# A hybrid diffusion step on one core: mixer B's first preparation placed in mixer A's tail, modulation with its weights stationary, substitution in two parts

## The chip, the cores and the metric

The kernel runs on one core of a Trainium2 chip. The metric is the device time of one execution in microseconds; lower is better. One execution was also profiled: that run's time and the span of its trace (first to last instruction) are given beside the runs that were only timed.

## What is computed

Two layers of a diffusion network are applied to a prompt of 128 tokens and a sample of 1024 (9 tiles of 128 tokens), model width 1024, all in fp32. The parts that the change touches belong to the first layer, and its modulation also to the second:

```python
def modulation(cvec, ada_w, ada_b):            # per layer, for the prompt and for the sample
    m = silu(cvec) @ ada_w + ada_b             # ada_w: 1024 x 3072
    return split_cols(m, [D_MODEL] * 3)        # shift, scale, gate

def even_layer(x, shift, scale, gate, ...):
    h = rms_norm(x, norm_pre) * (1 + scale) + shift
    qa, ka, va, ga, pb, gb = split_cols(h @ w_in, ...)
    ya = windowed attention with a sink        # mixer A, 8 heads
    yb = rwkv_mix(pb, ...)                     # mixer B, 8 heads, both directions in time
    y = concat(ya * silu(ga), yb * silu(gb)) @ w_out
    return x + gate * rms_norm(y, norm_post)

def rwkv_scan(S0, r, decay, kk, a, k, v, reverse):
    def step(S, inp):                          # one token
        sa = einsum('bhvk,bhk->bhv', S, -kk_t)
        S = S * w_t + outer(sa, kk_t * a_t) + outer(v_t, k_t)
        return S, einsum('bhvk,bhk->bhv', S, r_t)
```

The second layer is a differential attention over the same tokens.

## The kernel before

Projections are exact to fp32 by splitting operands into a high and a low fp32r part, three matmuls in place of one (L364 to L366, L378 to L380).

**Start.** `mod_chunks` computes the modulation in blocks of 128 of the 3072 columns. One step loads the weights (tiles `adaw`, from `in_ada_w`), then for each block 8 matmuls accumulate over the 1024 rows (L298). Their stationary operand is a 128 wide slice of the silu'd vectors `sc`, of which the first two columns count; the 128 columns of the weights stream past. The result has the vectors along partitions, so ScalarE copies it to SBUF (L300, tile `mrow`, or `raw` for four blocks in mixer A's tail), TensorE transposes it (L304) and VectorE adds the bias (L309 to L313). Sixteen blocks are needed before the first projection, four (`EARLY`) come behind mixer A, and 28 more, as a filler called `mods`, run along mixer B.

**Mixer A** runs in `mixer_a`, interleaved with the projections of `transposed`, whose weights are the tiles `wgh`, `wgl` (pool `wp`, two buffers; the four late modulation blocks use them too); A's own projection weights are `wa`, in the same pool. Its end is `values`: transposes of the probabilities (L652), products (L663, L664) in the bank `po`, and a gated copy (L672).

**Mixer B** cuts the tokens into chunks of 64 and solves each chunk as a triangular system. Work is divided into 9 items: for each of four pairs of heads the first and the second half of the sample's time, then the prompt for all. An item goes through these generators; each `yield` ends a step:

- `b_prep(item, direction)`, 5 steps: loads `low`, `lora` (one buffer each) and four `hb` tiles, two low-rank products (L943), tanh (L950), a running sum of the decay on VectorE (L960, one `tensor_tensor_scan` over 512 columns; the mask `rmask` restarts it every 64), exponentials and products.
- `b_front(item, direction)`, 10 steps, two halves: transposes (L1017), chunk products (L1027), masks (L1033 writes `za`, L1035 writes `q`), products (L1042).
- `b_subst(item)`, 2 steps: GpSimd gathers the diagonal blocks of `za` (L1061, four copies), VectorE transposes them so that columns lie along the free axis (L1062, tile `mp`, 32 columns), then GpSimd substitutes backward, 31 pairs of instructions (L1069, L1071) on the tile `rp`.
- `b_invert(item)`, 8 steps: VectorE transposes `rp` twice (L1077 into `Rt`, L1080), TensorE builds the rest of the inverse and the factors `E`, `VU`.
- `b_scan`: 8 serial steps over the chunks, in each TensorE (L1165), VectorE (L1167), TensorE (L1169), VectorE (L1176), ScalarE (L1178, the new state `S`).
- `b_finish`: normalization and gate, after the second half of each pair.

**What sets the order.** The generators are emitted by `timeline`: each part is given a start and an end in units of the iteration, its steps are spread evenly over them, and they are emitted in order of those times. Iteration i holds the scan of item i, the inversion of i + 1, fronts and substitution of i + 2, and the first preparation of i + 3; `TIMES` has a row for i = -2, i = -1, i = 0 to 4 and the rest, `T7` and `T8` serve the last two. The order of emission is a priority: a list scheduler then places instructions on the in-order queues of the engines by its own model, and may pass an instruction that it thinks is not ready. Tiles of closed pools are reused by later pools; an instruction that first touches such memory waits for the last reader there. SP issues nearly all loads, in its own order.

The four PSUM pools of mixer A lie from bank 0 as projection (2 banks), transposes (3), scores (2), output (1); mixer B's `ps_y` takes three banks from the other end, so its first tiles lie where A's output and scores were.

Of the kernel before, what the change touches and what calls it, by code (L numbers as in the profile page):

```python
# [19 lines left out]
P = 128  # L20
D = 1024
KT = D // P
# [119 lines left out]
def hybrid_step(ctx: ExitStack, tc: tile.TileContext, I, O, stop=99):  # L142
# [95 lines left out]
    def silu2(pool, x, out, tag="sge"):  # L238

        e = tl(pool, [P, x.shape[1]], tag, bufs=2)  # L240
        AE.activation(e, x, AF.Tanh, scale=0.5)
        VE.scalar_tensor_tensor(out, e, 1.0, x, op0=ALU.add, op1=ALU.mult)  # L242
# [33 lines left out]
    silu2(cp, cin, cin)  # L276
# [10 lines left out]
    def mod_chunks(l, c, n, pool, psum, tag, rows, bufs=2, ahead=None, tags=("adaw",) * 2):  # L287
# [36 lines left out]
    def mod_gate(l, psum, tag, rows):  # L324
# [3 lines left out]
        row = rows()[:16, :P]  # L328
# [370 lines left out]
    with ExitStack() as ph1:  # L699
        hp = ph1.enter_context(space("hT0", 1))  # L700
        hh, hl = tl(hp, [P, KT, TOK], "hh", F32R), tl(hp, [P, KT, TOK], "hl", F32R)
        with ExitStack() as su:
            xp = su.enter_context(space("su", 2))
            pt = su.enter_context(space("psut", 3, space=PSUM, side="right"))
            ps = su.enter_context(space("psu", 3, space=PSUM, side="right"))
# [10 lines left out]
            def chunks(j):  # L716
                ahead = []
                for _ in mod_chunks(0, 4 * j, 4, xp, ps, "ps", lambda: tl(xp, [P, P], "mrow"), 4, ahead):
                    pass
                ahead.pop()()  # L720
# [10 lines left out]
            for i in range(3):  # L731
# [20 lines left out]
        rest = transposed(blocks, wp, rp, bp, psum[0], psum[1], hh, hl, ind)  # L752
        run(some(rest, 7), 1, None, 1)
        run(rest, 56, hurried(mixer_a(hh, hl, wp, rp, ap, psum, rope, idb, msk), 1000), 12 * NT * 1)
        for c in range(16, 16 + EARLY):
            run(mod_chunks(0, c, 1, wp, psum[0], "ps", lambda: tl(rp, [P, 1024], "raw")[:, :P], tags=("wgh", "wgl")),
# [111 lines left out]
    NHB = 11  # L868
    ON_VE = ()
# [9 lines left out]
    class Item:  # L879
# [3 lines left out]
        def __init__(s, pairs, start, first=True, last=True):  # L883
            s.pairs, s.start, s.first, s.last = pairs, start, first, last
            s.nl = len(pairs)
            s.steps = 8 // s.nl

# [29 lines left out]
    def b_prep(it, d, pool, pre, ps_y, rmask):  # L917
# [42 lines left out]
        VE.tensor_tensor_scan(G, rmask, G, 0.0, op0=ALU.mult, op1=ALU.add)  # L960
# [89 lines left out]
    def b_subst(it, pool, pre, eye, eng):  # L1050
# [3 lines left out]
        mp, rpb = tl(pre, [P, 32, 32], "mp"), tl(pre, [P, 16, 32], "rp")  # L1054
        tmp = tl(pre, [P, 136], "tmp")
# [6 lines left out]
        VE.transpose(mp.rearrange("p c i -> p (c i)"),  # L1062
                     dg.rearrange("p (o u) c -> p c o u", o=1).to_broadcast([P, 32, 2, 16]))
        yield
        for j in range(31, 0, -1):
            t = j // 2
            n = 16 - t
            tv = tmp[:, :n * j].rearrange("p (t i) -> p t i", i=j)
            eng.tensor_tensor(tv, mp[:, j:j + 1, 0:j].to_broadcast([P, n, j]),  # L1069
                             rpb[:, t:16, j:j + 1].to_broadcast([P, n, j]), ALU.mult)  # L1070
            eng.tensor_tensor(rpb[:, t:16, 0:j], rpb[:, t:16, 0:j], tv, ALU.add)  # L1071
        it.rpb = rpb

    def b_invert(it, Rt, pool, pre, ps_s, ps_a):

        rpb, za = it.rpb, units(it)
# [174 lines left out]
    with ExitStack() as ph2:  # L1251
# [8 lines left out]
        ps_y = early.enter_context(space("bpy", 3, space=PSUM, side="right"))  # L1260
        ps_a = early.enter_context(space("bpa", 1, space=PSUM, side="right"))
        ps_s = ph2.enter_context(space("bps", 2, space=PSUM))
        ps_b = ph2.enter_context(space("bpb", 1, space=PSUM))
# [16 lines left out]
        rmask = tl(bc, [P, 512], "rmask")  # L1280
# [584 lines left out]
```

## Time and profile before

| | us |
|---|---|
| runs that were timed | 2103.79, 2097.02, 2094.81 (median 2097.02) |
| the profiled execution | 2095.15 |
| its span | 2093.3 |

| engine | busy, us | share of the span | instructions |
|---|---|---|---|
| TensorE, matmuls | 1966.0 | 94% | 15196 |
| TensorE, weight loads | 1789.1 | 85% | 15196 |
| VectorE | 1483.8 | 71% | 3758 |
| ScalarE | 1071.1 | 51% | 2856 |
| GpSimd | 685.6 | 33% | 951 |

TensorE's mean granted clock is 0.981 of full speed. The engines run side by side, each through its own queue in order; a busy share over the whole span is a mean over stages with different limits. In the rows below PE is TensorE's matmuls, PEld its weight loads, DVE VectorE, ACT ScalarE, POOL GpSimd, SPq the queue that issues loads.

### The profile page before, as it was taken

To read this page: it belongs to the slowest core of one execution; us is meant where nothing else is said; L and a number is where in the kernel's file an instruction comes from. 1 tells how busy PE (TensorE), PEld (TensorE's weight loads), DVE (VectorE), ACT (ScalarE), POOL (GpSimd) and SP (SyncE) were. 2 spreads that over 40 slices of the span, in tenths; PEclk is the share of its full clock that TensorE was granted. 3 is DMA by queue.
4 is the path that set the end of the run, shared out by engine and by line. 5 is a ranking of instruction groups with operands and counts; after the bars stand their busy time and mean duration, and the time that the engine had idled before them with its cause. 6 is when DMAs were issued, how large, how long until landed. Compare 5 with 4: busy or idle time off the path is not lost. (4 is left out here: it accounts for less than half of the span.)

```text
span 2093.3 us, 40906 instructions
## 1 busy us (share of the span) xinstructions
PE 1966.0 (94%) x15196; PEld 1789.1 (85%) x15196; DVE 1483.8 (71%) x3758; ACT 1071.1 (51%) x2856; POOL 685.6 (33%) x951
## 2 busy tenths in 40 slices
PE   7899999999779999998998999999999999999998
PEld 7899999999668888777777888999998999898786
DVE  5355567565756777867468677888888878887867
ACT  4433345343546555655356565555555555555643
POOL 1232232331176766656123222222222221212204
PEclk9999999999989999989999999999999999999999
DMA  7512233111654555433466410010101010101325
GB/s 288 162 62 74 65 96 104 63 56 50 201 168 150 162 165 156 138 113 120 156 213 232 144 37 29 31 31 28 32 28 40 20 45 15 50 10 48 105 66 177
DMA packets 165080, 205.72 MB, mean 98 GB/s; under 512 B 16369, under 2 KB 108049, under 8 KB 164881
## 3 DMA queue, kind: packets, MB, share of 16 engines
q1 hardware_dynamic: 162016, 198.25, 29.7%
q10 hardware_dynamic: 2864, 4.85, 0.7%
q8 instruction: 120, 1.97, 0.4%
q14 instruction: 80, 0.65, 0.1%
HBM read 152.32 MB, written 50.74 MB: 97 GB/s over the span
## 5 line engine op out<-in xcount | busy, mean ns | idle before, releaser
L1539 ACT ACTIVATE p<-s,mx 128x384 f32<-128x384 f32 (+1 forms) x400 | 225.1, 572 | 122.1 <-DVE mx L1536 99.7
L1534 DVE TENSOR_REDUCE mc<-s 128x1 f32<-128x384 f32 x384 | 204.7, 552 | 28.5 <-PE s L1532 25.0
L364 PE MATMUL ps<-wch,hh 128*128 128x384 f32 x576 | 205.0, 357 | 1.8 <-ACT wch L270 0.7
L1532 PE MATMUL s<-kst,qs 128*128 128x384 f32 x768 | 194.9, 353 | 10.1 <-ACT p L1539 9.7
L365 PE MATMUL ps<-wcl,hh 128*128 128x384 f32 x576 | 198.8, 345 | 4.7 <-POOL wcl L271 4.7
L366 PE MATMUL ps<-wch,hl 128*128 128x384 f32 x576 | 196.4, 341 | 2.7 <-DVE hl L1684 2.7
L411 POOL TENSOR_TENSOR q<-ropea,ropeb 128x256 f32<-128x256 f32 x56 | 44.1, 787 | 444.9 <-DVE ropeb L408 304.3
L378 PE MATMUL ps<-hh,wgh 128*128 128x384 f32 x504 | 173.4, 344 | 7.0 <-DVE bo L242 5.9
L379 PE MATMUL ps<-hl,wgh 128*128 128x384 f32 x504 | 172.5, 342 | 0.1
L380 PE MATMUL ps<-hh,wgl 128*128 128x384 f32 x504 | 171.5, 341 | 0.0
L1069 POOL TENSOR_TENSOR tmp<-mp,rp 128x126 f32<-128x126 f32 (+22 forms) x279 | 133.3, 478 | 63.2 <-DVE mp L1062 39.9
L1532 PEld LDWEIGHTS s<-kst,qs 128*128 128x128 f32 x768 | 127.3, 189 | 24.4 <-ACT p L1539 17.1
L271 POOL TENSOR_TENSOR wgl<-raw,wgh 128x1024 fp32r<-128x1024 f32 (+1 forms) x39 | 74.9, 1923 | 217.1 <-ACT wgh L270 216.9
L1071 POOL TENSOR_TENSOR rp<-rp,tmp 128x126 f32<-128x126 f32 (+22 forms) x279 | 129.5, 464 | 21.9
L1415 ACT CAST ah<-pt 128x512 fp32r<-128x512 f32 (+2 forms) x168 | 86.2, 533 | 79.2 <-PE pt L1570 77.1
L1416 DVE TENSOR_TENSOR al<-pt,ah 128x512 fp32r<-128x512 f32 (+2 forms) x168 | 100.7, 615 | 32.1 <-ACT ah L1415 30.8
L365 PEld LDWEIGHTS ps<-wcl,hh 128*128 128x128 f32 x576 | 109.2, 190 | 7.8 <-POOL wcl L271 7.3
L364 PEld LDWEIGHTS ps<-wch,hh 128*128 128x128 f32 x576 | 109.3, 190 | 5.9 <-DVE vl L1416 2.4
L366 PEld LDWEIGHTS ps<-wch,hl 128*128 128x128 f32 x576 | 109.1, 189 | 3.4 <-DVE hl L1684 3.4
L378 PEld LDWEIGHTS ps<-hh,wgh 128*128 128x128 f32 x504 | 94.9, 188 | 9.0 <-DVE bo L242 6.8
L271 POOL TENSOR_TENSOR wcl<-raw,wch 128x512 fp32r<-128x512 f32 x54 | 76.0, 1415 | 81.2 <-ACT wch L270 81.1
L1552 DVE SCALAR_TENSOR_TENSOR p<-p,lr,p 128x1152 f32<-128x1152 f32 (+1 forms) x72 | 98.9, 1374 | 0.4
(472 smaller groups left out, 5759.1 us busy)
## 6 DMA issues: line engine op xcount, KB each, us to landing
hb<-pbT SPq DMA_DIRECT2D x90, 256.0 KB, 4.1
adaw<-in_ada_w_dram SPq DMA_DIRECT2D x56, 256.0 KB, 3.7
raw<-in_wc_dram SPq DMA_DIRECT2D x48, 256.0 KB, 2.7
adaw<-in_ada_w_dram SPq DMA_DIRECT2D x8, 1024.0 KB, 10.5
pbT<-bm SPq DMA_DIRECT2D x16, 512.0 KB, 2.7
low<-lowT SPq DMA_DIRECT2D x16, 512.0 KB, 4.7
raw<-in_wo_dram SPq DMA_DIRECT2D x32, 256.0 KB, 2.8
raw<-in_wpb_dram SPq DMA_DIRECT2D x13, 512.0 KB, 3.6
```

The source lines that it names most:

```text
L271: eng.tensor_tensor(lo[:, j:j + w], raw[:, :w], hi[:, j:j + w].bitcast(F32), ALU.subtract)
L364: PE.matmul(ps[:, :n], hh[:, k, s], wh[:, k], start=k == 0, stop=False)
L365: PE.matmul(ps[:, :n], hh[:, k, s], wl[:, k], start=False, stop=False)
L366: PE.matmul(ps[:, :n], hl[:, k, s], wh[:, k], start=False, stop=k == KT - 1)
L378: PE.matmul(ps[:, :THIRD], wh[:, k], hh[:, k, s], start=k == 0, stop=False)
L379: PE.matmul(ps[:, :THIRD], wh[:, k], hl[:, k, s], start=False, stop=False)
L380: PE.matmul(ps[:, :THIRD], wl[:, k], hh[:, k, s], start=False, stop=k == KT - 1)
L1069: eng.tensor_tensor(tv, mp[:, j:j + 1, 0:j].to_broadcast([P, n, j]), rpb[:, t:16, j:j + 1].to_broadcast([P, n, j]), ALU.mult)
L1071: eng.tensor_tensor(rpb[:, t:16, 0:j], rpb[:, t:16, 0:j], tv, ALU.add)
L1532: PE.matmul(s[c][:, :w], qs[:, e, z], hd.kp[:, z] if own else hd.kst[:, z, w * c:w * c + w], start=e == 0, stop=e == 1)
L1534: VE.tensor_reduce(mc[:, c:c + 1] if nb > 1 else mx, s[c][:, :w], axis=AX.X, op=ALU.min)
L1539: AE.activation(e[:, w * c:w * c + w], s[c][:, :w], AF.Exp, scale=-1.0, bias=mx, accum_out=sums[:, z, c:c + 1])
```

## The change

1. `mod_chunks` swaps its operands: the weights become stationary and the slice of `sc` streams. The result stands with its columns along partitions, and the copy and the transpose go.
2. Mixer A's PSUM pools change places, the projection weights of `transposed` and of the late modulation blocks get a pool `wq` below A's `wa`, the start's PSUM pools move to the other side, and the first preparation of B (item 0, direction 0) gets two banks of its own, where the projections' banks were. B's other PSUM pools are opened behind it.
3. `b_subst` is cut in two: 24 of the 32 columns are transposed and substituted first, the other 8 columns have their own transpose, and their 7 pairs of steps are emitted when the item's inversion begins or the next item's substitution starts its steps, whichever is emitted first. `rp` gets two buffers.
4. The running sum of the decay is made in four pieces of 128 columns, and its mask is 128 wide.
5. `TIMES`, `T7` and `T8` get new values.

```diff
-            pr = tl(psum, [P, 512], tag)[:, 0:P]
+            ps = tl(psum, [P, 512], tag)
             for k in range(KT):
-                PE.matmul(pr, sc[:, 2 * k:2 * k + P], w[k // 4][:, k % 4, P * i:P * i + P], start=k == 0, stop=k == KT - 1)
-            row = rows()
-            AE.copy(row, pr)
-
-            def finish(i=i, row=row):
-                ps = tl(psum, [P, 512], tag)[:, 0:P]
-                PE.transpose(ps, row, ident)
-                ps = ps[:, 0:2]
+                PE.matmul(ps[:, 0:P], w[k // 4][:, k % 4, P * i:P * i + P], sc[:, 2 * k:2 * k + P], start=k == 0,
+                          stop=k == KT - 1)
+
+            def finish(i=i, ps=ps[:, 0:2]):
...
-            pt = su.enter_context(space("psut", 3, space=PSUM, side="right"))
-            ps = su.enter_context(space("psu", 3, space=PSUM, side="right"))
+            pt = su.enter_context(space("psut", 3, space=PSUM))
+            ps = su.enter_context(space("psu", 3, space=PSUM))
...
+        wq = ph1.enter_context(space("wq", 2))
         wp = ph1.enter_context(space("wp", 2))
         psum = [ph1.enter_context(space(n, b, space=PSUM))
-                for n, b in (("ppr", 2), ("ptr", 3), ("psc", 2), ("ppo", 1))]
+                for n, b in (("psc", 2), ("ppo", 1), ("ptr", 3), ("ppr", 2))]
+        psum = psum[3], psum[2], psum[0], psum[1]
...
-        rest = transposed(blocks, wp, rp, bp, psum[0], psum[1], hh, hl, ind)
+        rest = transposed(blocks, wq, rp, bp, psum[0], psum[1], hh, hl, ind)
...
+    SPLIT = 8
...
-        VE.tensor_tensor_scan(G, rmask, G, 0.0, op0=ALU.mult, op1=ALU.add)
+        for x in range(0, 512, P):
+            VE.tensor_tensor_scan(G[:, x:x + P], rmask, G[:, x:x + P], 0.0, op0=ALU.mult, op1=ALU.add)
...
+        it.rpb = rpb = tl(pre, [P, 16, 32], "rp", bufs=2)
...
+        def columns(a, b):
+            m = tl(pre, [P, b - a, 32], f"mp{a}")
+            VE.transpose(m.rearrange("p c i -> p (c i)"),
+                         dg[:, :, a:b].rearrange("p (o u) c -> p c o u", o=1).to_broadcast([P, b - a, 2, 16]))
+            return m
+
+        def steps(m, a, b):
+            for j in range(b - 1, max(a, 1) - 1, -1):
+                t = j // 2
+                n = 16 - t
+                tv = tl(pre, [P, 136], "tmp")[:, :n * j].rearrange("p (t i) -> p t i", i=j)
+                eng.tensor_tensor(tv, m[:, j - a:j - a + 1, 0:j].to_broadcast([P, n, j]),
+                                 rpb[:, t:16, j:j + 1].to_broadcast([P, n, j]), ALU.mult)
+                eng.tensor_tensor(rpb[:, t:16, 0:j], rpb[:, t:16, 0:j], tv, ALU.add)
+
+        high_columns = columns(SPLIT, 32)
+        yield
+        if it.before is not None:
+            it.before.last_steps()
+        low_columns = columns(0, SPLIT)
+        steps(high_columns, SPLIT, 32)
+        it.pending = lambda: steps(low_columns, 0, SPLIT)
+        yield
 
     def b_invert(it, Rt, pool, pre, ps_s, ps_a):
 
+        it.last_steps()
...
-        run(prep(0, 0), 1, None, 1)
+        with space("bpp", 2, space=PSUM, side="right") as ps_p:
+            for d in range(1):
+                run(b_prep(items[0], d, pool, fr, ps_p, rmask), 1, None, 1)
+        ps_y = early.enter_context(space("bpy", 3, space=PSUM, side="right"))
...
```

Each row of `TIMES` lists scan, inversion, finish, front 0, preparation 1, front 1, substitution, next preparation 0, the number of modulation steps and their time:

```diff
-        T7, T8 = ((-0.45, 0.93), (0.92, 1.54), (-0.16, 0.18)), (0.15, 0.54)
+        T7, T8 = ((-0.71, 0.77), (0.92, 1.55), (-0.2, 0.14)), (0.41, 0.8)
         TIMES = (
-            ((0.17, 0.93), (0.38, 1.09), (0.04, 0.46), (0.11, 0.32), (0.03, 0.3), (0.39, 0.75), (0.84, 0.85), (0.55, 1.18), 3, (0.04, 0.97)),
-            ((-0.17, 0.69), (0.79, 1.09), (-0.04, 0.37), (0.22, 0.32), (0.09, 0.4), (0.36, 0.72), (0.78, 0.79), (0.8, 1.29), 12, (0, 1)),
-            ((-0.01, 0.85), (0.6, 1.52), (-0.04, 0.48), (0.04, 0.32), (0.1, 0.38), (0.36, 0.69), (0.73, 0.83), (0.73, 1.23), 8, (0.0, 1.0)),
-            ((-0.16, 0.85), (0.48, 1.51), (-0.07, 0.44), (0.04, 0.32), (0.07, 0.38), (0.34, 0.71), (0.84, 0.96), (0.54, 1.16), 8, (0.01, 1.02)),
+            ((0.17, 1.0), (0.38, 1.09), (-0.04, 0.46), (0.11, 0.32), (0.05, 0.3), (0.39, 0.78), (0.84, 0.85), (0.55, 1.18), 4, (0.05, 0.97)),
+            ((-0.17, 0.69), (0.79, 1.09), (-0.04, 0.37), (0.22, 0.32), (0.09, 0.4), (0.36, 0.79), (0.78, 0.79), (0.64, 1.29), 12, (-0.31, 0.93)),
+            ((-0.05, 0.85), (0.6, 1.63), (0.27, 0.75), (0.04, 0.32), (0.1, 0.38), (0.36, 0.64), (0.79, 0.8), (0.54, 1.24), 7, (0.01, 0.97)),
+            ((-0.2, 0.85), (0.48, 1.62), (0.21, 0.71), (0.04, 0.32), (0.07, 0.38), (0.34, 0.66), (0.83, 0.84), (0.35, 1.17), 6, (0.02, 0.94)),
```

## Rows read from the trace of the kernel before

**Rows 1.** Busy time by stretch: PE, PEld, DVE, ACT, POOL, granted clock, DMA share, GB/s

```profile
60.00:540.00 480.00, 468.32 (x2924) 449.36 (x2923) 278.48 (x684) 189.97 (x434) 129.25 (x104) 1.00 0.27 88
540.00:634.00 94.00, 68.79 (x788) 57.52 (x786) 61.08 (x117) 44.43 (x119) 47.92 (x102) 0.85 0.58 181
634.00:983.00 349.00, 320.65 (x4545) 278.50 (x4544) 261.73 (x579) 200.41 (x521) 223.67 (x459) 0.97 0.46 142
983.00:1100.00 117.00, 112.70 (x888) 89.94 (x888) 71.49 (x169) 52.15 (x115) 31.09 (x48) 0.99 0.57 182
```

**Rows 2.** Timeline and one stretch around the end of mixer A

```profile
539.63 1.06 PE L298 MATMUL ps<-wgl,prm 128*128 128x128 f32 x8
...
540.71 0.59 SPq L929 DMA_DIRECT2D low<-lowT  x1
...
549.59 1.16 PE L943 MATMUL py<-low,lora 128*128 128x512 f32 x4 [1.97 <-DVE gt L672]
...
550.78 0.54 SPq L929 DMA_DIRECT2D low<-lowT  x1
...
556.39 2.05 PE L943 MATMUL py<-low,lora 128*128 128x512 f32 x4 [5.64 <-DMA lora<-loraT]
...
540.00:550.00 10.00, 6.21 (x33) 4.02 (x32) 8.34 (x21) 3.17 (x10) 1.17 (x2) 1.00 0.51 145
```

**Rows 3.** Timeline, item 0 from its substitution to its first state, all engines

```profile
577.09 3.29 POOL L1061 COPY hb<-za 32x512 f32<-32x512 f32 x4 [23.31 <-DVE za L1033]
...
613.15 0.23 POOL L1071 TENSOR_TENSOR rp<-rp,tmp 128x16 f32<-128x16 f32 x1
613.45 2.56 POOL L1061 COPY hb<-za 32x512 f32<-32x512 f32 x4
...
616.04 1.93 DVE L1062 STREAM_TRANSPOSE mp<-hb 128x1024 f32<-128x1024 f32 x1 [1.58 <-POOL hb L1061]
617.89 0.67 DVE L1080 STREAM_TRANSPOSE hb<-Rt 128x512 f32<-128x512 f32 x1
...
616.08 0.47 PE L304 MATMUL py<-cst,mrow 128*128 128x128 f32 x1 [8.42 <-ACT mrow L300]
...
634.26 0.68 ACT L1178 ACTIVATE S<-G,D 128x128 f32<-128x128 f32 x2
```

**Rows 4.** Busy time by stretch, two items of seven, from first state to first state

```profile
634.00:679.00 45.00, 43.24 (x651) 38.62 (x651) 31.37 (x67) 27.29 (x73) 27.64 (x56) 1.00 0.44 131
...
930.00:983.00 53.00, 46.28 (x623) 37.04 (x623) 41.99 (x99) 30.07 (x79) 36.94 (x80) 0.97 0.42 129
```

**Rows 5.** Groups of instructions, 634 to 983 us: busy, mean ns | idle before, releasers

```profile
L1069 POOL TENSOR_TENSOR tmp<-mp,rp 128x56 f32<-128x56 f32 (+22 forms) x216 | 106.5, 493 | 54.2 <-DVE mp L1062 37.9
...
L1061 POOL COPY hb<-za 32x512 f32<-32x512 f32 x28 | 17.0, 608 | 54.3 <-ACT mrow L300 30.1 <-PE sc L1165 8.3 <-ACT S L1178 8.0
```

**Rows 6.** Timeline, VectorE in one item, before the copies of 759.79 and behind

```profile
756.99 1.08 DVE L1077 STREAM_TRANSPOSE Rt<-rp 128x512 f32<-128x512 f32 x1
...
758.83 0.76 DVE L1033 TENSOR_TENSOR za<-pa,cstones 128x256 f32<-128x256 f32 x2
...
764.75 0.41 DVE L1167 TENSOR_TENSOR VU<-VU,sc 64x256 f32<-64x256 f32 x1 [2.66 <-PE sc L1165]
```

**Rows 7.** Timeline, TensorE at the start's last modulation block: start, duration, instruction

```profile
54.92 1.95 PE L298 MATMUL ps<-adaw,prm 128*128 128x128 f32 x16
...
58.00 0.27 PE L304 MATMUL ps<-cst,mrow 128*128 128x128 f32 x1
```

**Rows 8.** One line's instructions (min/median/max ns), then groups of 727 to 880 us

```profile
L304 PE MATMUL py<-cst,mrow x28: 272/328/475, 566.6 to 878.0; 128*128 128x128 f32 x28
...
L960 DVE TENSOR_TENSOR_SCAN hb<-rmask,hb x18: 1210/1225/1364, 551.6 to 941.5; 128x512 f32<-128x512 f32 x18
...
L1033 DVE TENSOR_TENSOR za<-pa,cstones 128x256 f32<-128x256 f32 x24 | 9.3, 417 | 0.8 <-PE pa L1027 0.6
...
L1035 DVE TENSOR_TENSOR q<-pa,cstones 128x512 f32<-128x512 f32 x12 | 8.2, 679 | 0.0
```

More of the change, by code (lines that the diff above doesn't have):

```diff
@@ L236, in some, with silu2 @@
             yield
-    def silu2(pool, x, out, tag="sge"):
-        e = tl(pool, [P, x.shape[1]], tag, bufs=2)
+    def silu2(pool, x, out, bufs=2):
+        e = tl(pool, [P, x.shape[1]], "sge", bufs=bufs)
         AE.activation(e, x, AF.Tanh, scale=0.5)
@@ L275, in hybrid_step @@
     cin = sc[:, :16]
-    silu2(cp, cin, cin)
+    silu2(cp, cin, cin, 1)
     VE.tensor_scalar(cin, cin, 0.5, None, op0=ALU.mult)
@@ L285, in hybrid_step, with mod_chunks @@
     gcol = tl(cp, [P, 2, 2, 8], "gcol")
-    def mod_chunks(l, c, n, pool, psum, tag, rows, bufs=2, ahead=None, tags=("adaw",) * 2):
+    def mod_chunks(l, c, n, pool, psum, tag, bufs=2, ahead=None, tags=("adaw",) * 2):
         w = []
@@ L327, in mod_gate @@
         PE.transpose(pt[:16, :P], gcol[:, l].rearrange("p r c -> p (r c)"), ident)
-        row = rows()[:16, :P]
+        row = rows()
         VE.tensor_copy(row, pt[:16, :P])
@@ L717, in chunks @@
                 ahead = []
-                for _ in mod_chunks(0, 4 * j, 4, xp, ps, "ps", lambda: tl(xp, [P, P], "mrow"), 4, ahead):
+                for _ in mod_chunks(0, 4 * j, 4, xp, ps, "ps", 4, ahead):
                     pass
@@ L886, in __init__, with last_steps @@
             s.steps = 8 // s.nl
+        pending = None
+        def last_steps(s):
+            if s.pending is not None:
+                s.pending()
+                s.pending = None
         def lanes(s, d):
@@ L1278, in ring @@
             return states[n][turn[n] % 3]
-        rmask = tl(bc, [P, 512], "rmask")
+        rmask = tl(bc, [P, P], "rmask")
         GE.memset(rmask, 1.0)
-        GE.memset(rmask[:, 0:512:64], 0.0)
+        GE.memset(rmask[:, 0:P:64], 0.0)
         items = []
@@ L1325, in hybrid_step @@
         for i, it in enumerate(items):
-            it.pool = pools[i % 3]
+            it.pool, it.before = pools[i % 3], items[i - 1] if i else None
             it.done = it.prev.done if not it.first else set()
-        rows = lambda: tl(fr, [P, P], "mrow")
-        T7, T8 = ((-0.45, 0.93), (0.92, 1.54), (-0.16, 0.18)), (0.15, 0.54)
+        rows = lambda: tl(fr, [16, P], "mrow")
+        T7, T8 = ((-0.71, 0.77), (0.92, 1.55), (-0.2, 0.14)), (0.41, 0.8)
         TIMES = (
[4 rows of a table removed]
[4 rows of a table added]
         )
@@ L1340, in mods @@
                 for c in range(a, 24):
-                    yield from mod_chunks(l, c, 1, fr, ps_y, "py", rows)
+                    yield from mod_chunks(l, c, 1, fr, ps_y, "py")
                 mod_gate(l, ps_y, "py", rows)
         mod, done = mods(), None
-        run(prep(0, 0), 1, None, 1)
+        with space("bpp", 2, space=PSUM, side="right") as ps_p:
+            for d in range(1):
+                run(b_prep(items[0], d, pool, fr, ps_p, rmask), 1, None, 1)
+        ps_y = early.enter_context(space("bpy", 3, space=PSUM, side="right"))
+        ps_a = early.enter_context(space("bpa", 1, space=PSUM, side="right"))
+        ps_s = ph2.enter_context(space("bps", 2, space=PSUM))
+        ps_b = ph2.enter_context(space("bpb", 1, space=PSUM))
         for i in range(-2, len(items)):
```

18 lines of the change are left out of this document (1 added, 17 removed).

## The prediction, made before the change ran

> **What bounds the kernel now.** I read the stretches first, the waits second, the order of single instructions last. The profiled execution took 2095.15 us, 2093.3 of them span; the median of the runs shown is 2097.02, 1.87 higher. The sum is made against 2095.15 and 1.87 is added at its end.
>
> The stretches [rows 1] show four regimes. Up to 60 us weights arrive and the modulation is computed. From 60 to 540 TensorE is busy 468.3 of 480 us: whatever delays its start there delays the end. From 540 to 634 mixer A ends and mixer B fills its pipeline: TensorE is busy 68.8 of 94 us, no engine is full, and the granted clock falls to 0.85. From 634 to 983 the first seven items of B are scanned. The change touches the first, third and fourth, and little behind.
>
> In the third regime the first preparation of B waits for mixer A's last instruction: its first matmul (L943) starts at 549.59, released by the VectorE instruction that last reads mixer A's output bank [rows 2]. The second preparation reuses the tile "low", so its load is issued only at 550.78, and its matmul starts at 556.39. Everything up to the first scan hangs on this chain: the copies for the substitution start on GpSimd at 577.09, its last step at 613.15; only then comes the inversion, and the first state of the scan is written at 634.26 [rows 3].
>
> In the fourth regime an item takes 45 to 53 us, from its first state to the next item's, of which the shortest and one of the longest of seven are shown [rows 4]. GpSimd works on the substitutions nearly in turn, but waits twice per item [rows 5]: before the copies (54.3 us over seven items, 7.8 each) and for the transposed columns (37.9 us, 5.4 each). The detail shows why [rows 6]: the mask of the second half of the next item (L1033) stands on VectorE behind the two transposes of the inversion of the item before, which themselves wait for the substitution before; and the transpose for GpSimd stands behind a scan update that waits 2.66 us for TensorE.
>
> **The change, part by part.**
>
> *Modulation.* Operands change places: 8 matmuls per column block stay, of the same two 128-wide operands, so I cost the matmuls at nothing. Removed are, per block, a ScalarE copy and a TensorE transpose. At the start this takes away the last block's way from its last matmul (54.92 + 1.95 = 56.87) to the end of its transpose (58.00 + 0.27), 1.4 us [rows 7], and sixteen transposes, at most 16 x 0.272 = 4.4 us of TensorE, of which I count 0.6. I take -2.0; bounds 0 and -5.8. The regime behind it has no slack, so all of it arrives.
>
> In B 28 blocks lose a transpose of 0.328 us [rows 8], 9.2 us of TensorE in all, and a ScalarE copy each, which I leave out: ScalarE is busy 57% there [rows 1]. Were TensorE the bound, all 9.2 would count: its matmul rows are busy 92% of 634 to 983. But its weight loads are busy 278.5 of 349 us, 80% [rows 1], and GpSimd and VectorE both have waits for order, so I take a third, -3.0; bounds 0 and -9.2. The Trainium skill, Trainium Kernel Development and Optimization, section Best Practices, says that the weight loads' share and not the matmuls' tells how full TensorE is. By that rule the engine has a fifth to spare and the sum stays at a third or less; by the matmul rows it would be the full saving.
>
> *First preparation in the tail of A.* Moved are its two loads ("low", "lora"; the four loads of its operands are early already), 4 matmul pieces, six ScalarE instructions, and eight VectorE ones with a memset. Now it needs two banks of the projection pool, which the last modulation block leaves at 539.63 + 1.06 = 540.69, and SBUF under the weights of A's projection instead of under the modulation's weights: the load of "low" is issued at 540.71, just as those are read for the last time [rows 2]. SP has nothing else to pass there but one store of mixer A's result. So the first matmul can start at 541.3 instead of 549.59, 8.3 us earlier. Not all arrives: the preparation has some 5.7 us of VectorE work, an estimate (the scan of 1.225, six of 512 columns at 0.68 each [rows 8] and a smaller one), and VectorE is busy 8.3 of the 10 us from 540 to 550 with A's last probabilities [rows 2]; what does not fit there delays A's last tile or itself. The second preparation then comes some 5 to 6 us earlier, and the chain behind it with it. I take -5.5; bounds 0 and -8.3. A's tail may end later at no cost, as long as the front's transposes find work: its last consumer is the output projection, hundreds of us later.
>
> *Substitution in two parts.* The number of steps stays, 31 pairs. One transpose, 1.93 us where it is seen alone [rows 3], becomes two (24 and 8 columns): by width 1.45 and 0.48, with a second start, which I leave in the bounds. GpSimd can start 0.5 us earlier per item. What is queued behind: for item 0 the new emission puts the copies of item 1 (613.45, 2.56 us) before the last 7 step pairs of item 0, so its inversion waits 2.6 us longer on GpSimd; in exchange VectorE is no longer held between the two transposes of the inversion (the second starts at 617.89, behind the transpose for item 1 at 616.04), and TensorE no longer sits 8.42 us at a modulation transpose that waits for ScalarE (616.08) [rows 3]; the modulation work that then falls into the inversion can be done in that idle time. I take -1.5; bounds +2.6 and -4.6. For later items the inversion is emitted ahead of the next copies, so GpSimd's order stays as it is.
>
> *Scan in four pieces.* 18 instructions of 1.225 us [rows 8] become 72 of a quarter of the width. The nearest pair of widths is the two masked copies L1033 and L1035: 0.417 us at 256 columns and 0.679 at 512 [rows 8], so 0.155 is fixed. Three more starts cost 0.47 us per scan, 8.4 in all. VectorE is busy 75% of the fourth regime; a third of it on the path, +2.8. Bounds 0 and +8.4. The smaller mask's memset is GpSimd work in a stretch where GpSimd idles, and costs nothing.
>
> *Order of B.* The second front's steps now end before the inversion's first step in the emitted order (its ninth of ten steps, the mask of the second half, at 0.36 + 0.8 x 0.28 = 0.584 against the inversion's 0.60; before at 0.36 + 0.8 x 0.33 = 0.624), so the mask need not stand behind the two transposes: 756.99 to 758.83, 1.8 us per item [rows 6], and with the 0.5 us of the shorter transpose 2.3 us. Against that, the transpose for GpSimd is emitted later (0.79 against 0.73), behind the scan's last step and the next preparation's first two. I take 0.85 us per item for seven items, -6.0; bounds -16 (2.3 x 7) and +34 (see the slower rival). The same retiming in items 7 and 8 lies in a stretch where TensorE is busy 112.7 of 117 us [rows 1]: at most 4.3 either way, taken as 0. Modulation blocks now reach one item further; they are filler and cost nothing while TensorE has a fifth to spare, else the same work.
>
> Sum: -2.0 - 3.0 - 5.5 - 1.5 + 2.8 - 6.0 = -15.2, so 2080.0 against the profiled execution and 2081.8 on the median. About 0.5%, 10.5 us, is what a measurement here can tell from no change.
>
> **The rivals.**
>
> *The order closes GpSimd's waits* (0.16): front and copies no longer depend on the inversion, and the period falls by the whole 2.3 us. For it speaks the item of [rows 6], where nothing but the order puts the mask behind the inversion; against it, that VectorE runs without a gap between the two. 2097.0 - 2 - 8.3 - 4.6 - 3 + 2.8 - 16 = 2066.
>
> *Only the pipeline's fill is gained* (0.20): item period as before, since the scan's own chain and VectorE set it. 2097.0 - 2 - 5.5 - 1.5 + 2.8 = 2091.
>
> *The move does nothing* (0.09): the preparation is placed early, but the fronts' banks, which mixer A's transposes hold to the end, or VectorE hold the chain where it was, and the steps of B gain nothing. 2097.0 - 2 + 2.8 = 2098.
>
> *Slower* (0.09): the transposes that feed GpSimd move behind the scan's last step and the preparation's first: 2.66 us of waiting [rows 6], 0.4 and four scan pieces of 0.46, 4.9 us per item. If GpSimd's cycle sets the period, seven items pay 34 us: 2097.0 - 9.2 + 34 = 2122. It decides from 2.8 us per item on, where it has eaten the -9.2 of the other parts and 10.5 more.
>
> **How the numbers follow.** The forecast has 0.46, its own range 2076 to 2088. Faster by over 0.5% (below 2086.5) are nine tenths of it and the first rival: 0.57. Within 0.5% are the rest, the second and the third rival: 0.34. Slower: 0.09. The range, 2064 to 2101, takes in the forecast and three rivals and leaves out the slower one and the tails.
>
> **What would show it.** Right: the first L943 matmul near 541, the second near 550; the first scan state near 626; no mrow copies; the scan as 72 instructions of some 0.4 us; GpSimd's two waits together well under 13 us per item and items of 48 to 49 us. Wrong: the first copies for the substitution still at 577 (the move does nothing); the period unchanged with shorter GpSimd waits (only the fill); the wait for the transposed columns over 8 us per item (slower).

## The result, and the profile after

The changed kernel takes 2085.14 us, the median of five runs (2079.10 to 2088.66), against 2098.01 for the kernel before in the same group: a ratio of 0.992, with an interval from 0.9894 to 0.9947. It is faster by about 0.8% by this ratio, and by 13 us between the medians. The profiled execution took 2079.22 us, 2077.4 of them span; its mean granted clock is 0.984, against 0.981.

The first view is the busy time by stretch, after, with the columns of [rows 1]; the second the same view cut at the first states of the items, items 0 to 6.

```profile
60.00:540.00 480.00, 467.27 (x2913) 449.51 (x2911) 279.94 (x680) 188.06 (x427) 128.89 (x104) 1.00 0.28 90
540.00:634.00 94.00, 75.09 (x824) 62.12 (x822) 66.90 (x143) 44.82 (x115) 46.81 (x98) 0.89 0.61 183
634.00:983.00 349.00, 320.98 (x4619) 277.56 (x4617) 270.93 (x641) 200.62 (x514) 229.66 (x500) 0.99 0.48 144
...
630.70:673.70 43.00, 41.69 (x636) 36.45 (x634) 31.96 (x74) 26.89 (x71) 31.18 (x70) 1.00 0.47 144
673.70:716.20 42.50, 40.55 (x635) 36.43 (x635) 33.74 (x77) 23.33 (x59) 27.25 (x60) 1.00 0.50 146
716.20:770.80 54.60, 48.80 (x675) 41.89 (x675) 43.67 (x109) 32.05 (x82) 32.01 (x68) 0.97 0.54 169
770.80:814.00 43.20, 41.15 (x641) 36.71 (x640) 34.02 (x77) 23.43 (x61) 28.86 (x66) 1.00 0.49 147
814.00:867.60 53.60, 46.92 (x672) 40.22 (x671) 43.23 (x109) 31.54 (x80) 31.58 (x67) 1.00 0.55 170
867.60:912.40 44.80, 40.53 (x628) 35.51 (x624) 35.02 (x79) 25.90 (x73) 31.62 (x72) 1.00 0.42 121
912.40:964.70 52.30, 46.39 (x625) 37.38 (x625) 40.87 (x100) 31.00 (x81) 35.01 (x75) 0.97 0.39 117
```

Of the 15.9 us between the two profiled executions, 3.6 were gained before the first state (630.7 after, 634.3 before [rows 3]) and 14.8 in the seven items (334.0 after, 348.8 before); 2.5 were lost again behind them. Short items and long ones alternate now: a long one also holds the finish of an earlier item. In a short one TensorE is busy 95% of the time (40.55 of 42.50). Two items of the kernel before, in the same view, stand against the second and the sixth line:

```profile
679.40:727.00 47.60, 44.66 (x664) 39.65 (x663) 35.34 (x75) 27.32 (x71) 33.29 (x69) 1.00 0.49 151
...
880.50:930.00 49.50, 43.93 (x600) 38.34 (x598) 32.66 (x69) 28.48 (x76) 26.77 (x60) 0.86 0.34 102
```

The end of mixer A after the change (the timeline; in the kernel's new line numbers L949 is the low-rank product, L967 the running sum, L634 and L668 are mixer A's, L1067 the copies, L1199 the state), to be read against [rows 2, 3]:

```profile
541.22 1.17 PE L949 MATMUL py<-low,lora 128*128 128x512 f32 x4
...
543.96 1.04 DVE L967 TENSOR_TENSOR_SCAN hb<-rmask,hb 128x128 f32<-128x128 f32 x3
...
548.16 1.21 DVE L978 TENSOR_TENSOR zr<-hb,hb 128x512 f32<-128x512 f32 x1
549.30 0.74 DVE L634 TENSOR_SCALAR p<-p,li 128x384 f32<-128x384 f32 x2
...
549.76 1.54 PE L648 MATMUL pt<-cst,p 128*128 128x128 f32 x6 [6.24 <-DVE p L634]
...
554.92 1.31 PE L949 MATMUL py<-low,lora 128*128 128x512 f32 x4
...
556.50 0.43 DVE L668 SCALAR_TENSOR_TENSOR gt<-po,gt 64x256 f32<-64x256 f32 x1
...
578.70 3.28 POOL L1067 COPY hb<-za 32x512 f32<-32x512 f32 x4 [14.91 <-DVE za L1040]
...
630.65 0.75 ACT L1199 ACTIVATE S<-G,D 128x128 f32<-128x128 f32 x2
```

The first preparation starts where it was expected, 8.4 us earlier. But its VectorE work stands between mixer A's last softmax steps: the last scaling of the probabilities (L634) runs at 549.30, TensorE waits 6.24 us for it, and the second preparation's product stands on TensorE's queue behind A's last products, at 554.92, 1.5 us earlier than before. The first copies for the substitution are 1.6 us later than before: by the prediction's own sign (copies still at 577) the move did nothing.

GpSimd's two waits (the groups of 634 to 983 us) answer to [rows 5]: 54.5 + 27.9 us against 54.3 + 37.9. The wait ahead of the copies has hardly moved, but most of it is now for another thing, a reader of an `hb` tile:

```profile
L1081 POOL TENSOR_TENSOR tmp<-mp,rp 128x126 f32<-128x126 f32 (+22 forms) x236 | 100.6, 426 | 45.8 <-DVE mp L1072 27.9
L1067 POOL COPY hb<-za 32x512 f32<-32x512 f32 x28 | 19.6, 701 | 54.5 <-DVE zr L977 31.5 <-DVE rst L251 10.1 <-DMA rp<-in_cst_dram 6.1
```

### The profile page after: what moved, and what is told of

The parts are those of the page before. It is cut to its first block, busy times and chain, and to the rows that moved or that the text cites. A ratio compares the mean times of both kernels' runs of the same rounds, so it can differ in the third digit from the quotient of the medians.

```text
span 2077.4 us, 40804 instructions
## 1 busy us (share of the span) xinstructions
PE 1952.1 (94%) x15148; PEld 1777.4 (86%) x15148; DVE 1488.3 (72%) x3821; ACT 1058.8 (51%) x2808; POOL 673.6 (32%) x951
## 5 line engine op out<-in xcount | busy, mean ns | idle before, releaser
L1081 POOL TENSOR_TENSOR tmp<-mp,rp 128x126 f32<-128x126 f32 (+22 forms) x279 | 117.8, 422 | 52.3 <-DVE mp L1072 31.1
```

The lines of the kernel that those rows point to most:

```text
L1081: eng.tensor_tensor(tv, m[:, j - a:j - a + 1, 0:j].to_broadcast([P, n, j]), rpb[:, t:16, j:j + 1].to_broadcast([P, n, j]), ALU.mult)
```

## The experiments

Each kernel was timed beside the kernel before, in one of three groups on different chips, so kernels of different groups are compared by their ratios to it; 0.001 of a ratio is 2.1 us, and a difference of two ratios is uncertain by some 7 us. "Seven items" is the time from the first state of item 0 to that of item 7 in the profiled execution.

**The changed kernel again**, with no edit, beside the others of its group.

> The changed kernel, run again beside the others of this group so that they can be held against it on the same chip. Its ratio to the kernel before was 0.992 with an interval from 0.9894 to 0.9947, so 0.990 to 0.995 again.

Measured: 2083.76 us, 0.9931 (0.9907 to 0.9955). Its profiled execution was the slowest of its ten: first state 639.1, seven items 337.5 us. The changed kernel thus stands at 0.992 to 0.993.

**The new times undone.**

```diff
-        T7, T8 = ((-0.71, 0.77), (0.92, 1.55), (-0.2, 0.14)), (0.41, 0.8)
+        T7, T8 = ((-0.45, 0.93), (0.92, 1.54), (-0.16, 0.18)), (0.15, 0.54)
...
```

> The changed kernel with the old TIMES, T7 and T8; modulation, the first preparation in the tail, the split substitution and the scan in four pieces stay. Theory (the new order gave the 14.8 us that seven items became shorter): the items from the first state on are back at 49 to 50 us each (seven in 344 to 349 us), the first state stays near 631, and the time is 12 to 16 us above the changed kernel, 2096 to 2101. Rival (the items became shorter because 28 transposes left TensorE and the substitution's low columns left GpSimd's path): seven items stay at 334 to 338 us and the time at 2084 to 2090.

Measured: 2092.60 us, 0.9983 (0.9959 to 1.0006); first state 634.4, seven items 349.7 us. Without the order the rest of the change brings 0.2%, 0.4% at most by the interval, not told from nothing; the 11 to 13 us that are lost are most of the gain. With the old times GpSimd's copies wait mainly for the mask (`za`), as the prediction had it:

```profile
L1067 POOL COPY hb<-za 32x512 f32<-32x512 f32 x28 | 17.3, 619 | 71.7 <-DVE za L1040 46.1 <-ACT S L1199 14.4 <-issue 10.4
```

**The new times alone**, in the kernel before.

```diff
-        T7, T8 = ((-0.45, 0.93), (0.92, 1.54), (-0.16, 0.18)), (0.15, 0.54)
+        T7, T8 = ((-0.71, 0.77), (0.92, 1.55), (-0.2, 0.14)), (0.41, 0.8)
...
```

> The kernel before with the new TIMES, T7 and T8 and nothing else of the change. Theory (the order alone carries it): seven items in 333 to 340 us in place of 348.8, first state near 634, time 2083 to 2090. Rival (the order needs the substitution in two parts, since its first part must not hold the transposes for GpSimd): seven items at 345 us or more and the time at 2094 or above; it may be slower than before, because the transposes that feed GpSimd are emitted later.

Measured: 2082.43 us, 0.9940 (0.9917 to 0.9963); seven items 332.4 us. The order does it alone; it needs neither the split nor the other form of the modulation. What inside the order does it comes below.

**The early preparation undone.**

```diff
-        with space("bpp", 2, space=PSUM, side="right") as ps_p:
-            for d in range(1):
-                run(b_prep(items[0], d, pool, fr, ps_p, rmask), 1, None, 1)
...
         ps_b = ph2.enter_context(space("bpb", 1, space=PSUM))
+        run(prep(0, 0), 1, None, 1)
...
-                for n, b in (("psc", 2), ("ppo", 1), ("ptr", 3), ("ppr", 2))]
-        psum = psum[3], psum[2], psum[0], psum[1]
+                for n, b in (("ppr", 2), ("ptr", 3), ("psc", 2), ("ppo", 1))]
...
-        wq = ph1.enter_context(space("wq", 2))
```

> The changed kernel with the first preparation of B behind the opening of B's banks again, mixer A's banks in the old places and the projection weights in one pool with A's. Theory (the move is worth the 3.6 us by which the first state came earlier): first low-rank matmul near 549.5, first state near 634, the items unchanged, the time 3 to 4 us above the changed kernel, 2088 to 2089. Rival (the move is worth nothing or costs, since it delays A's probabilities and the second preparation): first state at 629 to 631 and the time at 2082 to 2085. Third reading (the early start was what the fill was gained by, 8 us): 2093.

Measured: 2076.57 us, 0.9900 (0.9876 to 0.9923), if anything 4 to 7 us faster than the changed kernel, and faster than any of the three readings; first state 631.3, seven items 339.1 us. The 3.6 us of the profiled execution are not the move's. The stretch from 540 us to the first state, here, after, and in the second profile of the changed kernel (one line each), and last the second profile's first low-rank product:

```profile
540.00:631.30 91.30, 69.31 (x795) 57.69 (x793) 62.29 (x133) 43.22 (x112) 44.35 (x97) 0.89 0.65 195
```

```profile
540.00:630.70 90.70, 71.94 (x802) 59.76 (x800) 63.67 (x136) 43.45 (x112) 43.91 (x93) 0.89 0.60 181
```

```profile
540.00:639.10 99.10, 80.87 (x826) 68.14 (x824) 66.91 (x145) 45.56 (x118) 47.09 (x101) 0.81 0.56 171
```

```profile
544.57 1.17 PE L949 MATMUL py<-low,lora 128*128 128x512 f32 x4
```

At a granted clock of 0.89 the stretch takes 91 us with the move or without it; the same kernel at 0.81 takes 99. Of these 8.4 us, 3.3 had passed before B's first product (544.57 against 541.22), so at most 5 go with the clock behind it.

**The old form of the modulation** in the changed kernel.

```diff
-                PE.matmul(ps[:, 0:P], w[k // 4][:, k % 4, P * i:P * i + P], sc[:, 2 * k:2 * k + P], start=k == 0,
+                PE.matmul(pr, sc[:, 2 * k:2 * k + P], w[k // 4][:, k % 4, P * i:P * i + P], start=k == 0, stop=k == KT - 1)
+            row = rows()
+            AE.copy(row, pr)
...
+                PE.transpose(ps, row, ident)
```

> The changed kernel with the old form of the modulation: vectors stationary, a ScalarE copy, a transpose back. Theory (TensorE isn't full in B and the start gave 0.9 us): 1 to 4 us above the changed kernel, 2086 to 2089, seven items 334 to 337 us. Rival (TensorE's transposes and their waits for ScalarE are what held the items): seven items at 343 us or more, 2094 or above.

Measured: 2086.34 us, 0.9960 (0.9944 to 0.9976), 6 to 8 us above the changed kernel by the ratios, with an interval that overlaps both of the changed kernel's. By the median that is the theory's time, by the ratios it lies between theory and rival. Seven items took 346.2 us in the profiled execution, as the rival has it, but that was the second slowest of twelve runs, at a granted clock of 0.95 in these items. So this run doesn't decide; the form is tried once more, without the other parts, in "Modulation and order alone".

**The substitution in one piece.**

```diff
-        high_columns = columns(SPLIT, 32)
+        all_columns = columns(0, 32)
         yield
-        if it.before is not None:
-            it.before.last_steps()
-        low_columns = columns(0, SPLIT)
-        steps(high_columns, SPLIT, 32)
-        it.pending = lambda: steps(low_columns, 0, SPLIT)
+        steps(all_columns, 0, 32)
```

> The changed kernel with the substitution in one piece again: one transpose of 32 columns, 31 pairs of steps in one go, one buffer of rp. Theory (the order of B carries the gain, and the split only spares part of a transpose): within 3 us of the changed kernel, the first state 629 to 633, seven items 332 to 338 us. Rival (the split lets GpSimd take the next item's copies while the inversion waits, so the new order needs it): the gap ahead of the copies grows by 4 us per item and seven items take 345 us or more, 2094 or above.

Measured: 2084.22 us, 0.9930 (0.9909 to 0.9951); first state 635.6, seven items 335.1 us. The split is worth nothing that shows.

**The running sum in one piece**, with the substitution in one piece.

```diff
-        for x in range(0, 512, P):
-            VE.tensor_tensor_scan(G[:, x:x + P], rmask, G[:, x:x + P], 0.0, op0=ALU.mult, op1=ALU.add)
+        VE.tensor_tensor_scan(G, rmask, G, 0.0, op0=ALU.mult, op1=ALU.add)
```

> The run with the substitution in one piece, and also the running sum of the decay in one instruction of 512 columns with a mask as wide. Against that run (0.993 of the kernel before): the prediction's term says 2.8 us less for one piece, at most 8.4; if the start of an instruction is hidden or costs nothing more, the difference is under 1 us. By its rows one whole sum should take 1.225 us and the four pieces 1.36 to 1.37 together, so 18 x 0.14 = 2.5 us of VectorE, of which a third counts: about 1 us.

Measured: 2083.55 us, 0.9939 (0.9916 to 0.9962), seven items 333.0 us: no gain from one piece. One line's instructions (min/median/max ns), here and after, and then one sum in four pieces in the timeline after:

```profile
L966 DVE TENSOR_TENSOR_SCAN hb<-rmask,hb x18: 1206/1225/1452, 548.2 to 929.2; 128x512 f32<-128x512 f32 x18
```

```profile
L967 DVE TENSOR_TENSOR_SCAN hb<-rmask,hb x72: 390/414/694, 544.0 to 921.9; 128x128 f32<-128x128 f32 x72
```

```profile
613.21 1.37 DVE L967 TENSOR_TENSOR_SCAN hb<-rmask,hb 128x128 f32<-128x128 f32 x4
```

The record of one piece lasts 0.414 us, but four behind one another take 1.37 in all: the records overlap, and the price is 0.14 us per sum, not the 0.47 of the prediction.

**Modulation and order alone**: both the edits above and the early preparation undone.

```diff
-        for x in range(0, 512, P):
-            VE.tensor_tensor_scan(G[:, x:x + P], rmask, G[:, x:x + P], 0.0, op0=ALU.mult, op1=ALU.add)
+        VE.tensor_tensor_scan(G, rmask, G, 0.0, op0=ALU.mult, op1=ALU.add)
...
+        run(prep(0, 0), 1, None, 1)
```

> Of the change only the modulation's new form and the new times: the substitution and the running sum in one piece, the first preparation behind the opening of B's banks, mixer A's banks and weights in their old places. If the other three parts are worth nothing together, as the runs that undid one each suggest, 0.989 to 0.994 of the kernel before, as fast as the changed kernel or faster; if the early preparation's 3.6 us reach the end, 3 to 4 us more than the run with the whole sum, with the first state near 634.

Measured: 2084.41 us, 0.9944 (0.9919 to 0.9970); first state 638.1 at a clock of 0.81, seven items 332.7 us. Against the kernel with the new times alone (0.9940, 332.4 us) it differs in the form of the modulation only (and the tiles and banks that go with it): no difference.

**One new time undone: the second front.**

```diff
-(0.36, 0.64)
+(0.36, 0.69)
...
-(0.34, 0.66)
+(0.34, 0.71)
```

> The changed kernel with one of the new times put back: the end of the second front in iterations 0 to 6 (0.69 and 0.71 in place of 0.64 and 0.66), so that on VectorE the mask of the front's second half stands behind the first transpose of the inversion again. Theory (this is what the order gained by, as the prediction had it): the copies for the substitution wait for the mask again, seven items take 342 to 350 us in place of 334 to 338, and the time is 8 to 14 us above the changed kernel, 2091 to 2098. Rival (the finish, moved from the start of an iteration to its second half, is what counts): seven items 333 to 340 us and the time within 3 us.

Measured: 2087.97 us, 0.9972 (0.9950 to 0.9995), seven items 341.3 us. This one time costs 9 to 11 us by the ratios, uncertain by 7; the median is 3.7 us above that of the next kernel, of the same group. VectorE shows that the mask (L1040) stands behind the inversion's first transpose (L1098) again; the first two lines below are here, the second two of the changed kernel, where it runs ahead. But the copies do not wait for it, as the theory had it: for item 3 the timeline shows a wait for the load of `rp`, for item 4 one for an `hb` tile (the last two lines). By what path the later front costs time is open.

```profile
752.31 1.07 DVE L1098 STREAM_TRANSPOSE Rt<-rp 128x512 f32<-128x512 f32 x1
756.87 0.73 DVE L1040 TENSOR_TENSOR za<-pa,cstones 128x256 f32<-128x256 f32 x2
```

```profile
746.28 0.41 DVE L1040 TENSOR_TENSOR za<-pa,cstones 128x256 f32<-128x256 f32 x1
748.95 1.07 DVE L1098 STREAM_TRANSPOSE Rt<-rp 128x512 f32<-128x512 f32 x1
```

```profile
705.68 3.28 POOL L1067 COPY hb<-za 32x512 f32<-32x512 f32 x4 [4.07 <-DMA rp<-in_cst_dram]
763.12 3.94 POOL L1067 COPY hb<-za 32x512 f32<-32x512 f32 x4 [14.24 <-DVE hb L1251]
```

**Another new time undone: the finish.**

```diff
-(0.6, 1.63), (0.27, 0.75)
+(0.6, 1.63), (-0.04, 0.48)
...
-(0.48, 1.62), (0.21, 0.71)
+(0.48, 1.62), (-0.07, 0.44)
```

> The changed kernel with another of the new times put back: the finish of the item before in iterations 0 to 6 (from -0.04 and -0.07 to 0.48 and 0.44 in place of 0.27 and 0.21 to 0.75 and 0.71). Theory (the mask's place is what the order gained by): time within 4 us of the changed kernel, but the odd and even items are less unlike (the finish falls into the iteration's first half, where the front still works). Rival (moving the finish carries the gain): the copies for items 4 and 6 start as early as the masks allow, and yet seven items take 342 us or more and the time is 8 to 14 us above the changed kernel.

Measured: 2084.25 us, 0.9942 (0.9919 to 0.9965), seven items 339.2 us: the finish's place carries little or nothing that shows.

**A tile of its own for the copies.** In the timeline of the changed kernel the copies of items 4, 5 and 6:

```profile
757.42 3.70 POOL L1067 COPY hb<-za 32x512 f32<-32x512 f32 x4 [16.02 <-DVE zr L977]
796.61 2.55 POOL L1067 COPY hb<-za 32x512 f32<-32x512 f32 x4 [1.72 <-DVE za L1040]
854.70 3.70 POOL L1067 COPY hb<-za 32x512 f32<-32x512 f32 x4 [15.52 <-DVE zr L977]
```

```diff
-    NHB = 11
+    NHB = 10
...
-        dg = hb(pool, [P, 16, 32])
+        dg = tl(pool, [P, 16, 32], "dg", bufs=1)
```

> The changed kernel with a tile of its own for the diagonal blocks that GpSimd copies, and 10 in place of 11 hb tiles in the ring that they came from. In the changed kernel the copies of items 4 and 6 start at 757.4 and 854.7, 11 us after the masks that they read (746.7 for item 4), because the ring's next tile is still read by the finish of an earlier item or by a preparation. Theory (GpSimd's cycle of substitutions sets the period of two items, and this wait is its new gap): these copies start near 747 and 844 relative to the same first state, the two long items shrink by 4 to 9 us each, seven items take 318 to 328 us, and the time is 6 to 16 us below the changed kernel. Rival (VectorE's and TensorE's work sets the items in which an item is finished): the copies start earlier, but the states don't, seven items 331 to 337 us, and the time is within 3 us. Third reading (ten tiles are too few): preparations wait, and the time rises.

Measured: 2086.95 us, 0.9949 (0.9930 to 0.9967), seven items 344.5 us. The same three copies in the timeline, and then the long items 2 and 4 in the view by stretch:

```profile
750.01 2.56 POOL L1067 COPY dg<-za 32x512 f32<-32x512 f32 x4 [7.80 <-DVE za L1040]
803.48 2.56 POOL L1067 COPY dg<-za 32x512 f32<-32x512 f32 x4 [12.82 <-DVE za L1040]
849.40 2.56 POOL L1067 COPY dg<-za 32x512 f32<-32x512 f32 x4 [6.67 <-DVE za L1040]
```

```profile
721.70:778.10 56.40, 50.11 (x675) 42.67 (x674) 44.38 (x109) 31.77 (x81) 38.19 (x81) 0.94 0.51 159
821.50:878.20 56.70, 50.86 (x672) 43.82 (x672) 43.86 (x109) 31.30 (x79) 39.52 (x83) 0.91 0.52 158
```

The 16 us wait shrinks to 7.8, and the next grows from 1.72 to 12.82. What GpSimd gains in one item it waits for in the next, and the states come no earlier; the time is some 4 us above the changed kernel of the same group. So this wait isn't what sets the items. That some of a gain is hidden can't be excluded: the two long items ran at a lower granted clock, 0.94 and 0.91 against 0.97 and 1.00.

**The same with the substitution in one piece**, and 11 tiles in the ring.

```diff
-        dg = hb(pool, [P, 16, 32])
+        dg = tl(pool, [P, 16, 32], "dg", bufs=1)
...
-        high_columns = columns(SPLIT, 32)
+        all_columns = columns(0, 32)
```

> As the run with the tile of its own, but with the substitution in one piece and one buffer of rp, which makes room to keep 11 hb tiles. If the ring is what held the copies, this gains as much as with ten tiles, 6 to 16 us against the kernel with the substitution in one piece; if ten tiles are too few, this one alone gains; if VectorE or TensorE sets the period, neither does.

Measured: 2094.97 us, 0.9982 (0.9958 to 1.0005), slower than the kernel with the substitution in one piece (0.9930). So it was not that ten tiles are too few. A tile of its own costs 11 us here; seven items take 348.6 us, the two long ones at a granted clock of 0.88. Why the clock falls there is open.

No version beat the changed kernel by more than the intervals: the one with the early preparation undone has the lowest ratio, but its interval overlaps both of the changed kernel's.

### What the order gains

That the new times carry the gain is shown by two runs, with the times taken out of the changed kernel and with them alone. What inside the times does it is read from the traces. TensorE is the fullest engine in the items, so I follow its work: how much modulation an item holds, and at what clock.

The 28 blocks leave 16 records each on TensorE (every fp32 matmul leaves two). The view is that of L298's instructions alone, TensorE's matmuls and weight loads: first of the kernel before, items 0 to 4 and item 5; then of the new times undone, the same; then of the changed kernel.

```profile
634.30:880.50 246.20, 41.89 (x320) 37.53 (x320) 0.99 0.50 153
880.50:930.00 49.50, 0.00 (x0) 0.00 (x0) 0.86 0.34 102
```

```profile
634.40:881.40 247.00, 42.38 (x320) 37.77 (x320) 0.99 0.50 153
881.40:930.50 49.10, 0.00 (x0) 0.00 (x0) 0.82 0.36 109
```

```profile
630.70:867.60 236.90, 38.33 (x272) 34.07 (x272) 0.99 0.51 157
867.60:912.40 44.80, 4.55 (x32) 3.98 (x32) 1.00 0.42 121
```

The new counts in the times (7 and 6 steps per item in place of 8) take three blocks out of items 0 to 4 and put two into item 5, one ahead of the first state. All instructions of items 0 to 4, in the run with the new times undone and in the second profile of the changed kernel, which differ in the times alone:

```profile
634.40:881.40 247.00, 229.26 (x3297) 200.84 (x3296) 191.85 (x445) 136.23 (x345) 154.47 (x325) 0.99 0.50 153
```

```profile
639.10:877.30 238.20, 220.41 (x3254) 193.04 (x3252) 186.53 (x444) 137.23 (x348) 147.62 (x319) 0.99 0.51 156
```

The five items are 8.8 us shorter, and TensorE's busy time is 8.85 us shorter, at the same clock. The blocks explain only a part of it: by the lines of L298, TensorE's time with them fell by 3.6 us from before to after (41.89 to 38.33), though 48 records would be 6.3 us at the 0.131 us a record of the kernel before (41.89 / 320). The rest of the fall is in other records, whose number did not change (2977 and 2982 without L298). Nor do the blocks fix the length. In the last experiment above, items 0 to 4 hold the same 272 records of L298 as in the changed kernel, and take 248.2 us at a clock of 0.94 (the view of L298, then all instructions):

```profile
638.30:886.50 248.20, 38.10 (x272) 33.62 (x272) 0.94 0.49 149
```

```profile
638.30:886.50 248.20, 230.81 (x3255) 201.44 (x3253) 189.05 (x439) 137.42 (x349) 163.37 (x345) 0.94 0.49 149
```

Over all twelve profiles with the new times these five items take 235.9 to 248.2 us with 272 records each: up to 238.2 at a clock of 0.99, 236.8 to 242.0 at 0.97 and 0.98, 242.8 to 248.2 at 0.94 to 0.96. At 0.99 the old times took 246.2 and 247.0. So at an equal clock the new times are worth 8 to 11 us here, of which the blocks are 4 to 6 by their records; and as much again can go with a lower clock.

In item 5 it is the other way round: with two blocks more it takes 4.7 us less (44.8 against 49.5), and the granted clock no longer falls there as it did: 0.86 and 0.82 with the old times, 0.93 to 1.00 in all twelve profiles with the new ones, at 44.0 to 47.6 us. The Trainium skill, TensorE: Matmul & The Clock Gate, section What's actually happening, says that a throttled clock is the array's default and activity lifts it. The trace agrees as far as it goes: 600 matmul records in item 5 at the two lower clocks, 625 to 628 at the higher ones. That the two blocks did it is likely, but other times changed with them.

Over the 91 runs of the kernel before that stand beside these experiments, a line through time and mean granted clock gives 14.7 us for each 0.01. Their mean clock is 0.9743, that of 15 runs of the changed kernel 0.9787: 0.0044 x 1465 = 6.5 us, half of the 13.2 us between the means (2096.6 and 2083.5). This is an association and no second gain beside the first: item 5's clock is in it, and the line through the 15 runs of the changed kernel gives only 8.5 us for each 0.01.

The counts were not put back by themselves, so their share is not shown by a run; the two times that were put back, front and finish, leave item 5 at a clock of 1.00.

## Why the prediction was right, and where its steps failed

The time came out as forecast, 2085 against 2082, and the sum of -15.2 us against -15.9 in the profiled executions; the parts did not. Five of the six terms, -9.2 together, show as nothing or can't be told from it, and the sixth came out 5 to 7 us larger than taken. That these errors cancel is luck.

*Order of B*, -6.0: the term was too small. The runs give -11 to -13. Its mechanism was the mask ahead of the inversion. With the old times the copies do wait for the mask, 46.1 us over seven items, and in the changed kernel 1.7, so the order did what was foreseen. But nothing shows that the gain came by that wait: GpSimd's two waits together fell from 13.2 to 11.8 us per item ((54.5 + 27.9) / 7), not well under 13; the later front cost 4 to 11 us without the copies waiting for the mask; and taking the new wait away gained nothing. The term also counts seven items, though the mask moves ahead of the inversion in the times of iterations 0 to 4 only; in the row behind them it stays at 0.34 + 0.8 x 0.32 = 0.596, behind the inversion's 0.48.

The step that can't stand is "Modulation blocks now reach one item further; they are filler and cost nothing while TensorE has a fifth to spare". TensorE's busy time in items 0 to 4 and their length fell by the same 8.8 us, the blocks taken out being 4 to 6 of it by their records, and item 5 got shorter with two blocks more. No run isolates the blocks, so how much of the gain is theirs stays open.

That fifth came from the weight loads' share of 80% [rows 1]. In a short item after the change it is 86% (36.43 of 42.50) where matmuls fill 95%. By the rule of the Trainium skill, Trainium Kernel Development and Optimization, section Best Practices, which judges the distance to roofline by the weight loads' share and not the matmuls', a seventh would still have been free there. No run here shows that it was: where items got shorter, TensorE's busy time fell with them.

*First preparation in the tail*, -5.5: nothing. The first product came at 541.22, as foreseen; "The second preparation then comes some 5 to 6 us earlier" failed. The prediction saw that VectorE was full there and that A's tail may end later, and called that free; but the second preparation stands behind that tail on TensorE, at 554.92 in place of "near 550", and the first state came at 630.7 in place of 626. Of the rivals, "The move does nothing" had this part right.

*Modulation*, -2.0 at the start and -3.0 in B: nothing that shows at the start. With the early preparation undone, the two profiles with the new form have B's first product at 550.11 and 550.82, against 549.59 [rows 2] and 548.40 with the old one. In B two pairs of kernels disagree, 0 and 6 to 8 us; a difference of two ratios is uncertain by some 7, so a term of 3 stays open.

*Substitution in two parts*, -1.5, and *scan in four pieces*, +2.8: both 0 within 7 us, so terms of this size stay open too; the size of the second was taken from two other instructions, and its own rows show 0.14 us per sum in place of 0.47.

Of the rivals, "Only the pipeline's fill is gained" is contradicted most plainly: the fill gained nothing that lasts, the items the rest. The slower one did not come: the wait for the transposed columns fell from 5.4 to 4.0 us per item.

## What to carry to other kernels

When one engine is nearly full, count how much filler each period holds before looking at the waits of the others, and then put that count back by itself: here new times in the emission, filler counts among them, gained more than an early start, a split and a shorter form together, and which of the times did it was never isolated. An early start is worth what the second in line gains, so follow the queue one step further. And compare two profiles only beside their granted clocks: the same five items with as many blocks in them took 237 us in one of these kernels at 0.99, and 248 in another at 0.94.

## What was unexpected of the hardware

Item 5 was shorter with more work in it (628 records in 44.8 us at a clock of 1.00, against 600 in 49.5 at 0.86). Four scans of 128 columns behind one another took 1.37 us, though the record of each lasts 0.414 and one of 512 takes 1.225. GpSimd's four copies took 3.70 us in items 4 and 6, 3.28 and 2.92 in items 0 and 7, and 2.55 in the others; what slowed them was not tried.
